# Rotating keys, values and the meta block of a head group with VectorE's 32-block transpose and GpSimd transfers through DRAM

## The chip, the cores and the metric

The kernel runs on one core of one Trainium2 chip. The metric is the device time in microseconds (us) of one execution. A core has a matrix engine (TensorE, PE in the profile; its weight loads are listed as PEld), VectorE (DVE), ScalarE (ACT), GpSimd (POOL) and SyncE (SP), each with its own queue of instructions that it works off in order. Weights come from DRAM by transfers (DMA) that SP issues; GpSimd can issue transfers as well. PE works from SBUF, 128 partitions wide, into PSUM; ACT and DVE bring results from PSUM back to SBUF.

## The reference

One decoder block, width 2048, on 256 tokens with 16 learned meta tokens in front (272 in all). An RWKV-7 path and an attention path with forget gates (FoX), 16 heads of 64 each, run side by side on the same normalised input; their outputs are gated, added and projected, and a SwiGLU layer follows. All is float32.

```python
def _layer(h, ...):
    xn = _rms(h, n1)
    proj = xn @ w_in                       # 2048 x 10704
    z_rwkv, z_fox, z_gate = jnp.split(proj, (RWKV_COLS, RWKV_COLS + FOX_COLS), axis=-1)
    z_prev = jnp.pad(z_rwkv, ((0, 0), (1, 0), (0, 0)))[:, :-1]
    z_rwkv = z_rwkv + (z_prev - z_rwkv) * mu
    y_a = _rwkv7(z_rwkv, ...)              # per head: S = S*w + (S a) b' + v k',  y = S r
    y_b = _fox(z_fox, q_g, k_g, f_bias)    # softmax(q k' * scale + c_q - c_k, causal) v
    g_a, g_b = jnp.split(jax.nn.sigmoid(z_gate), 2, axis=-1)
    h = h + (g_a * (y_a @ w_a) + g_b * (y_b @ w_b)) @ w_o
    gate, up = jnp.split(_rms(h, n2) @ w_gu, 2, axis=-1)
    return h + (jax.nn.silu(gate) * up) @ w_dn
```

## The kernel before

**Precision and weights.** Each float32 matrix product is made of three products of a faster 32-bit type. A weight tile of 128 x 1024 (512 KB) is fetched by SP into `raw` (4 buffers), ACT copies its high part into `wh` (L353), DVE subtracts to get the low part `wl` (L354; 4 buffers each), and PE multiplies both with the activations (L383 to L385, or L459 and L461 where two terms share a matmul). Each weight element is used once, so the chain SP, ACT, DVE, PE runs from start to end of the kernel.

**Stages.** The projection goes head group by head group (four groups g of four heads). For each group the main work is: the RWKV columns k, v, r and the small low-rank products (`rwkv_jobs`, `lora`), the FoX columns q, k, v (`fox_jobs`), then two blocks of gate columns (`gate_jobs`, tile name `zg`). The first group starts some 50 us in and the last group's chain ends at about 560 us. Remaining gate blocks, the branch products, the output projection and the SwiGLU layer follow.

**What sets the order.** PE's order is written out by hand. Beside the main jobs there are background streams, Python generators `rwkv_bg` (L763) and `fox_bg` (L1132), one each per group. After every few main matmuls `slot` (L415) adds the matmuls' nominal time to a clock and, where a stream is due, lets it emit its next step. A stream yields how long it wants to be left alone in nominal ns: the constants `LANE`, `NORM`, `Y_...`, `X_...` at the top of the file. So the small matmuls of one group's recurrence and attention stand between the large ones of the next group's projection. The order on DVE, ACT and POOL is set by the framework's scheduler from priorities and modelled times, with semaphores for every dependence. An engine waits at the first instruction that is not ready, and everything behind it on that engine waits too.

**The steps that the change touches**, per group. `rwkv_bg` builds, from r, k and v after the token-shift (`lerp`, L500; its difference `zd` on POOL at L514, its end on DVE at L517) and the cumulated decay, the tiles `bk` (keys and b vectors, channels on partitions, 128 x 1024; `bk0` for the meta block), `ar`, and the products `NK` (PE `mat`, DVE L835 and L845). The recurrence needs keys and values with tokens on partitions. For that PE turns `bk` by 8 transposes of 128 x 128 against an identity (`trbk`), `v` by 4 (`trv`), and the meta block by 2 (`tr`), all through `pe_tr` (L411 to L413) at L883 to L908, and ACT brings them from PSUM into `BK` (two tags: `bt`), `SV` (`sv`), `BK0` and `SV0` (L891, L900, L905, L907). Then DVE inverts small triangular blocks in `lx` (L921 and L923), `lx` goes through DRAM into `X`, `X0` and `XL`, and the chain of `step` (L939) runs over the chunks with matmuls `rhs`, `u`, `s`, `y`; at its end `yT` is turned back on PE and put into `ya` (one half on ACT, L1050, one on DVE, L1052). `fox_bg` turns v of the attention (`vv`) by 4 PE transposes (`pv`) and its last 32 tokens (`ve`) by one (`pvm`) at L1132 to L1148; ACT scales them into `vt` and `vm`. After that come `biases` (POOL, L1163 to L1166), `scores` (PE `sc`, DVE sum and row maximum L1186, `nm` L1189, ACT exponentials), division (DVE L1203), transposes `ppt` and the product `po` with `vt` and `vm`.

That is 14 + 5 = 19 transposes by the identity per group, 76 in all.

Of the kernel before, what the change touches and what calls it, by code (L numbers as in the profile page):

```python
# [13 lines left out]
ALU = mybir.AluOpType  # L14
# [80 lines left out]
LANE = 24000  # L95
# [6 lines left out]
NORM = 5150  # L102
# [16 lines left out]
Y_AB = 6000  # L119
# [3 lines left out]
Y_TRBK = 1600  # L123
Y_TR0 = 2400
Y_RHS = 1400
Y_U = 1400
Y_XT = 800
Y_QT = 1200
Y_GN = 1400
# [5 lines left out]
def hybrid_block(ctx, tc, A, out, dbg=None):  # L135
# [626 lines left out]

    def rwkv_bg(g, box):  # L763
# [101 lines left out]
        nc.gpsimd.tensor_copy(bk0[:, :, 0, 32:32 + NMETA], vr[:, :, :NMETA])  # L865
# [28 lines left out]
        ps = aux_ps(f"trv{g}")  # L894
        for m in range(2):
            for e in range(2):
                i = 2 * m + e
                pe_tr(ps[:, i * P:(i + 1) * P], vr[:, m, NMETA + e * P:NMETA + (e + 1) * P], ident)
        for cc in range(2):
            nc.scalar.activation(SV[HD:, :, cc::2, :].rearrange("p h i d -> p i h d"),  # L900
                                 ps[hb(cc), :].rearrange("p (i h d) -> p i h d", h=2, d=HD), AF.Copy)
        ps = aux_ps(f"tr0{g}")
        for m in range(2):
            pe_tr(ps[:, m * P:(m + 1) * P], bk0[:, m].rearrange("p x t -> p (x t)"), ident)
        nc.scalar.activation(BK0.rearrange("p h m d -> p m h d"),  # L905
                             ps[:, 0:2 * P].rearrange("p (m h d) -> p m h d", h=2, d=HD), AF.Copy)
# [11 lines left out]
        for s_ in range(31):  # L918
# [20 lines left out]
        def step(c, S, BK, SV, NK, X, Y):  # L939
# [1209 lines left out]
```

## Time and profile before

| | |
|---|---|
| time, median of 3 (lowest to highest) | 1492.32 us (1492.18 to 1492.40) |
| the profiled execution: its time, its span | 1492.06 us, 1490.1 us |
| ACT busy | 844.3 us, 57% of the span |
| POOL busy | 157.0 us, 11% |
| moved by DMA | 307.63 MB, mean 206 GB/s |
| of it read from DRAM, written to it | 286.55 MB, 19.30 MB |

The profiled execution took 0.26 us less than the median, and 1.96 us of its time lie outside the span. The three runs lie within 0.22 us. In the rows that follow, "busy" is the time that an engine executed. Matmuls overlap in PE's pipeline, so the duration of one record is longer than the distance between the starts of two; where the cost of PE work is wanted, starts have to be compared. "Idle before" is the time in which an engine had nothing running just before an instruction of the group, with the instruction that released it.

### The profile page before, as it was taken

What the parts mean: (1) busy time and instruction counts of PE and PEld (TensorE: products, weight loads), DVE (VectorE), ACT (ScalarE), POOL (GpSimd) and SP (SyncE); (2) the same over time, 40 slices, a digit from 0 to 9 for tenths busy, and PEclk for the clock granted to TensorE, in tenths of its full rate; (3) what the DMA queues carried; (4) which work ended last, traced back from release to release, by engine and by line L of the source; (5) the groups of instructions that cost most, each with busy time, mean ns of one, the idle gap of its engine ahead of it and who ended that gap; (6) DMA issues with size and microseconds to landing.
All of it is one profiled execution on the core that took longest, in us unless ns stands there. A gap on an engine that the chain in (4) does not pass through costs nothing.

```text
span 1490.1 us, 27294 instructions
## 1 busy us (share of the span) xinstructions
PE 1480.7 (99%) x10371; PEld 1326.7 (89%) x10371; DVE 1246.3 (84%) x2154; ACT 844.3 (57%) x1255; POOL 157.0 (11%) x273
## 2 busy tenths in 40 slices
PE   9999999999999999999999999999999999999998
PEld 9999999989989888998888999999999988788886
DVE  7888699699789767776778788888898887999898
ACT  7664665575485455554555555555655555565554
POOL 2212202203212010000002000000000002221000
PEclk9999999999999999999999999999999999999999
DMA  8566556646636757767779655675666567988652
GB/s 275 171 178 191 153 146 188 173 140 174 193 114 180 223 148 230 238 219 244 258 252 342 206 176 195 200 244 184 207 230 208 198 213 221 315 265 264 218 198 85
DMA packets 226210, 307.63 MB, mean 206 GB/s; under 512 B 27232, under 2 KB 150128, under 8 KB 226080
## 3 DMA queue, kind: packets, MB, share of 16 engines
q1 hardware_dynamic: 209344, 277.39, 59.9%
q0 software_dynamic: 10688, 22.02, 4.5%
q10 hardware_dynamic: 6048, 6.49, 1.3%
q8 instruction: 81, 1.33, 0.4%
q14 instruction: 49, 0.40, 0.1%
HBM read 286.55 MB, written 19.30 MB: 205 GB/s over the span
## 4 chain that ended last, share of the span: by engine, by line
PE 85%; issue 12%; DVE 1%; DMA 1%; ACT 0%; POOL 0%; SPq 0%; DVEq 0%; POOLq 0%; ACTq 0%
PE zg L459 8%; PE up L459 5%; PE gt L459 5%; PE zg L461 4%; PE dn L1936 4%; PE dn L1935 4%; PE dn L1937 4%; PE up L461 2%; PE f L383 2%; PE gt L461 2%; PE f L385 2%; PE f L384 2%; PE f L459 2%; PE br L383 2%; PE br L384 2%
## 5 line engine op out<-in xcount | busy, mean ns | idle before, releaser
L354 DVE TENSOR_TENSOR wl<-raw,wh 128x1024 fp32r<-128x1024 f32 x268 | 326.6, 1226 | 91.7 <-ACT wh L353 87.1
L353 ACT ACTIVATE wh<-raw 128x1024 fp32r<-128x1024 f32 x268 | 281.7, 1057 | 196.4 <-PE br L384 36.2
L459 PE MATMUL zg<-xhl,wh 128*128 128x512 f32 x512 | 180.1, 398 | 0.0
L459 PE MATMUL gt<-hts,wh 128*128 128x512 f32 x512 | 179.3, 394 | 0.0
L459 PE MATMUL up<-hts,wh 128*128 128x512 f32 x512 | 179.3, 394 | 0.0
L1620 DVE TENSOR_TENSOR wl<-raw,wh 128x1024 fp32r<-128x1024 f32 x128 | 155.1, 1219 | 20.8 <-ACT wh L1617 16.4
L1617 ACT ACTIVATE wh<-raw 128x1024 fp32r<-128x1024 f32 x128 | 133.6, 1051 | 51.9 <-PE gt L459 11.9
L461 PE MATMUL gt<-hts,wl 128*128 128x256 f32 x480 | 134.4, 280 | 0.0
L461 PE MATMUL up<-hts,wl 128*128 128x256 f32 x480 | 134.3, 280 | 0.0
L461 PE MATMUL zg<-xhl,wl 128*128 128x256 f32 x480 | 134.3, 280 | 0.0
L1786 ACT ACTIVATE wh<-fr 128x1024 fp32r<-128x1024 f32 x48 | 50.9, 1061 | 112.9 <-DVE fr L1763 107.9
L459 PEld LDWEIGHTS zg<-xhl,wh 128*128 128x128 f32 x512 | 94.3, 188 | 19.1 <-issue 0.7
L459 PEld LDWEIGHTS up<-hts,wh 128*128 128x128 f32 x512 | 94.5, 188 | 17.2 <-DVE gates L1650 0.2
L459 PEld LDWEIGHTS gt<-hts,wh 128*128 128x128 f32 x512 | 94.5, 188 | 17.0
L1935 PE MATMUL dn<-wh,ach 128*128 128x512 f32 x242 | 95.0, 393 | 0.0
L1936 PE MATMUL dn<-wh,acl 128*128 128x512 f32 x242 | 94.9, 392 | 0.0
L1937 PE MATMUL dn<-wl,ach 128*128 128x512 f32 x242 | 94.7, 392 | 0.0
L461 PEld LDWEIGHTS zg<-xhl,wl 128*128 128x128 f32 x480 | 90.9, 189 | 1.1
L461 PEld LDWEIGHTS gt<-hts,wl 128*128 128x128 f32 x480 | 90.9, 189 | 1.0
L461 PEld LDWEIGHTS up<-hts,wl 128*128 128x128 f32 x480 | 90.9, 189 | 1.0
L1789 DVE TENSOR_TENSOR wl<-fr,wh 128x1024 fp32r<-128x1024 f32 x48 | 58.8, 1224 | 28.8 <-ACT wh L1786 25.6
L528 ACT ACTIVATE wh<-tt 128x1024 fp32r<-128x1024 f32 x44 | 46.7, 1062 | 61.3 <-PE dn L1936 48.3
(774 smaller groups left out, 4118.7 us busy)
## 6 DMA issues: line engine op xcount, KB each, us to landing
raw<-in_w_in_dram SPq DMA_DIRECT2D x160, 512.0 KB
raw<-in_w_gate_up_dram SPq DMA_DIRECT2D x128, 512.0 KB
fr<-in_w_gate_up_dram SPq DMA_DIRECT2D x96, 256.0 KB
raw<-in_w_down_dram SPq DMA_DIRECT2D x44, 512.0 KB
q<-in_w_down_dram SPq DMA_DIRECT2D x44, 512.0 KB
raw<-in_w_o_dram SPq DMA_DIRECT2D x32, 512.0 KB
raw<-in_w_branch_a_dram SPq DMA_DIRECT2D x16, 512.0 KB
raw<-in_w_branch_b_dram SPq DMA_DIRECT2D x16, 512.0 KB
```

The source lines that it names most:

```text
L353: nc.scalar.activation(th, rr, AF.Copy)
L354: nc.vector.tensor_tensor(tl, rr, th.bitcast(F32), op=ALU.subtract)
L383: nc.tensor.matmul(ps, wh, ah, start=first, stop=False)
L384: nc.tensor.matmul(ps, wh, al, start=False, stop=False)
L459: nc.tensor.matmul(ps.rearrange("p (a t) -> p a t", a=2), wh, act, start=first, stop=last)
L461: nc.tensor.matmul(ps[:, :T], wl, act[:, 0, :], start=False, stop=False)
L1617: nc.scalar.activation(w[0], raw[0].rearrange("p (k j c) -> p k j c", k=2, j=1), AF.Copy)
L1620: nc.vector.tensor_tensor(w[1], raw[0].rearrange("p (k j c) -> p k j c", k=2, j=1), w[0].bitcast(F32), op=ALU.subtract)
L1789: nc.vector.tensor_tensor(w[1], raw[0], w[0].bitcast(F32), op=ALU.subtract)
L1935: nc.tensor.matmul(o, a[0], hi, start=first, stop=False)
L1936: nc.tensor.matmul(o, a[1], hi, start=False, stop=False)
L1937: nc.tensor.matmul(o, a[0], lo_, start=False, stop=last)
```

## The change

The 76 transposes of keys, values and meta block leave PE, with ACT's copies out of PSUM (12 per group, the 2 into `ve` among them). In their place, per group:

- DVE runs nine 32 x 32-block transposes (`STREAM_TRANSPOSE`; `turned`): `bt` from `bk`, 128 x 1024; `sv` from `v`, twice 128 x 256; `t0` (meta block), three of 128 x 64; `vt` from `vv`, twice 128 x 256, and its last 32 tokens, 128 x 64. Within each 32 x 32 block, rows and columns are then swapped; the blocks themselves are still in the old place.
- POOL writes each result to DRAM (`bkd` 512 KB, `vd` 256 KB, `t0d` 96 KB, `vtd` 288 KB) and reads it back with the blocks moved: 4 transfers for `bk`, 2 for `SV`, 4 for `BK0`, 1 for `SV0`, 4 for `vv`, 2 for `vm`. These are 4 writes and 17 reads, 21 transfers that POOL issues per group, 84 in all, in rows of 128 B to 1 KB.
- POOL puts the columns in order: two copies into `bt`, four scalings into `vt`, one of `vm`; one more tile to clear (`BK0`), one copy less (`bk0` from v).

In the same edit the last `ya` copies move from DVE to ACT, four small `nm` products per pair of heads become one, `vv` is brought in once with 272 columns, `XL`'s transfers come last, `SV`'s and `vt`'s columns lie in blocks of 32, and some of the streams' delays change.

```diff
-LANE = 24000
+LANE = 25000
-NORM = 5150
+NORM = 7750
-X_DIV = 2600
-X_PT = 2350
-X_PT0 = 5750
+X_DIV = 3600
+X_PT = 3100
+X_PT0 = 6850
-Y_AB = 6000
+Y_AB = 5900
-Y_TRBK = 1600
-Y_TR0 = 2400
+Y_SOLVE = 4000
+V_LAND = 14050
-Y_XT = 800
+Y_XT = 900
-Y_GN = 1400
+Y_GN = 2200
...
+    def turned(tmp, srcs, dram):
+        for dst, src in srcs:
+            nc.vector.transpose(dst, src)
+        nc.gpsimd.dma_start(dram, tmp)
+
+    def rows_of(dram):
+        return dram.rearrange("(a i) b x -> b i a x", i=32)
...
-        nc.gpsimd.tensor_copy(bk0[:, :, 0, 32:32 + NMETA], vr[:, :, :NMETA])
+        BK, SV = (rw.tile([P, 4, 8, 32], F32, tag=t, name=f"{t}{g}", bufs=1) for t in ("bt", "sv"))
...
+        turned(bv, [(BK, bk.rearrange("p m c x (q j) -> p (x q) (m c) j", j=32))], bkd)
+        sv = SV[:, 0:2]
+        turned(sv.rearrange("p b i j -> p b (i j)"),
+               [(sv[:, :, 4 * m:4 * m + 4, :], vr[:, m, NMETA:].rearrange("p (c b j) -> p b c j", b=2, j=32))
+                for m in range(2)], vd)
+        turned(t0.rearrange("p b m j -> p b (m j)"),
+               [(t0[:, x], bk0[:, :, x, :32]) for x in range(2)] + [(t0[:, 2], vr[:, :, :32])], t0d)
...
-        for m in range(2):
-            ps = aux_ps(f"trbk{g}{m}")
-            for c in range(4):
-                pe_tr(ps[:, c * P:(c + 1) * P], bkf[:, 4 * m + c, :], ident)
-            nc.scalar.activation(BK[:, :, 4 * m:4 * m + 4, :].rearrange("p h c d -> p c h d"),
-                                 ps.rearrange("p (c h d) -> p c h d", h=2, d=HD), AF.Copy)
-        yield Y_TRBK
...
-        yield Y_TR0
-
+        yield Y_SOLVE
...
+            if s_ == 7:
+                bkx = bk.rearrange("p m c x t -> p (m c x t)")
+                for b in range(4):
+                    nc.gpsimd.dma_start(bkx[32 * b:32 * b + 32].rearrange("p (a x) -> p a x", a=4), rows_of(bkd)[b])
+                flat = lambda t: t.rearrange("p a i j -> p a (i j)")
+                for b in range(2):
+                    nc.gpsimd.dma_start(flat(SV[HD + 32 * b:HD + 32 * b + 32]), rows_of(vd)[b])
...
+        for h in range(2):
+            nc.gpsimd.tensor_copy(BK[:, h].rearrange("p i (q j) -> p q i j", j=32),
+                                  bkx.rearrange("p (h q i j) -> p h q i j", h=2, q=2, j=32)[:, h])
...
-                if h == cc:
-                    nc.scalar.activation(dst, src, AF.Copy)
-                else:
-                    nc.vector.tensor_copy(dst, src)
+                nc.scalar.activation(dst, src, AF.Copy)
...
-                pe_tr(pv_[:, t * 256 + m * P:t * 256 + (m + 1) * P], vv[:, m, t * P:(t + 1) * P], ident)
-        pe_tr(pvm[:4 * NMETA, :P], ve.rearrange("p m c -> p (m c)"), ident)
...
+        turned(vt.rearrange("p b m j -> p b (m j)"),
+               [(vt[:, t:8:2], vv[:, :, t * P:(t + 1) * P].rearrange("p m (b j) -> p b m j", j=32))
+                for t in range(2)] + [(vt[:, 8], vv[:, :, T - NMETA:])], vtd)
+        yield HOP
+        vb = vv.rearrange("p m l -> p (m l)")[:, :4 * P].rearrange("p (a x) -> p a x", a=4)
+        for b in range(4):
+            nc.gpsimd.dma_start(vb[32 * b:32 * b + 32], vtd[:, 2 * b:2 * b + 2].rearrange("(a i) t x -> i a (t x)", i=32))
...
+        yield V_LAND
         while len(ready) < 2 or not gate_done:
             yield X_V
...
+                nc.gpsimd.tensor_scalar(vt[:, t, m].rearrange("p h (q j) -> p h q j", j=32), v5[:, t, m],
+                                        rsk[:, t:t + 1], None, op0=ALU.mult)
+        nc.gpsimd.tensor_scalar(vm[:2 * NMETA], vm[:2 * NMETA], rsz, None, op0=ALU.mult)
...
-                    nc.vector.tensor_scalar(nm, nm, -1.0, r, op0=ALU.mult, op1=ALU.mult)
...
+            nc.vector.scalar_tensor_tensor(nm, nm, -1.0, hr.rearrange("p (t m h) -> p t m h", t=2, m=2)[:, :, m, :],
+                                           op0=ALU.mult, op1=ALU.mult)
```

Three places show what this does to the order. In the rows, the number behind a name tells apart tiles of one name, and the last figures are the shape.

On PE, before, where the first group's gate columns (`zg`) are multiplied while the group's keys and values are turned:

```order
L461 MATMUL zg_1_1585<-xhl,wl 128x256
L413 MATMUL trbk_1654<-ident,bk_1301 128x128 x4
L413 MATMUL trbk_1660<-ident,bk_1301 128x128 x4
L459 MATMUL zg_1_1585<-xhl,wh 128x512
L461 MATMUL zg_1_1585<-xhl,wl 128x256
```

The same place of the changed kernel, behind the sums `bs` that stand ahead of it in both:

```order
L900 MATMUL bs_1621<-rkl_1314,bones 128x256
L459 MATMUL zg_1_1600<-xhl,wh 128x512
L461 MATMUL zg_1_1600<-xhl,wl 128x256
L459 MATMUL zg_1_1600<-xhl,wh 128x512
L461 MATMUL zg_1_1600<-xhl,wl 128x256
```

The transposes are gone and nothing has taken their place; the two other places of the group (`pv` with `pvm`, and `trv` with `tr`) are emptied likewise.

On POOL, before, between the first group's bonus term `bo` and the difference `zd` of the second group's first key block, with what each waits for in brackets:

```order
L879 TENSOR_SCALAR bo_1600<-bo_1600,vcol 128x256 [waits DVE_49]
L1163 TENSOR_SCALAR b_1701<-bias_1700,cq,hs_999 128x144 [waits DMAHW4_49]
...
L1166 TENSOR_TENSOR bias_1700<-bias_1700,cmask 128x2x128 [waits Pool_49]
L805 MEMSET bk_2919 128x256 [waits PE_49]
L505 MEMSET z 128x1 [waits Activation_49]
L514 TENSOR_TENSOR zd<-z 128x272 [waits DVE_49,Activation_49,Pool_49]
```

The same stretch of POOL in the changed kernel, whose line numbers are higher by 15 to 25 there:

```order
L902 TENSOR_SCALAR bo_1615<-bo_1615,vcol 128x256 [waits DVE_49]
L931 DMA SV_1511<-t0d_1518 32x4x64 [waits DMASW5_49]
L766 DMA vtd_1647<-vt_1646 128x576 [waits DMASW6_49,DVE_49]
L940 COPY bt_1509<-bk_1300 128x2x8x32 [waits DMASW2_49,DMASW3_49,DMASW1_49,DMASW0_49]
L940 COPY bt_1509<-bk_1300 128x2x8x32
L813 MEMSET bk_2850 128x256 [waits PE_49]
L1155 DMA vv_997<-vtd_1647 32x4x128 [waits DMASW7_49,DMASW6_49,Activation_49]
...
L1166 TENSOR_SCALAR vt_1646<-vv_997,rsk 128x128 [waits DMASW2_49,DMASW7_49,DMASW1_49,DMASW0_49]
L1166 TENSOR_SCALAR vt_1646<-vv_997,rsk 128x128 x3
...
L514 TENSOR_TENSOR zd<-z 128x272 [waits DVE_49,Pool_49]
```

Ahead of `zd` now stand transfers, and instructions that wait for landings (the waits named DMASW are for transfers that POOL itself issued); the `biases` have moved behind the scalings of `vt`.

On DVE, before, at the change from the first to the second group: a weight subtraction, root steps of small vectors, the products `NK`, and the next weight subtraction:

```order
L354 TENSOR_TENSOR wl<-raw,wh 128x1024
L295 TENSOR_TENSOR ht<-hr_2496 128x8
L296 SCALAR_TENSOR_TENSOR ht<-hs_2495,ht 128x8
L297 SCALAR_TENSOR_TENSOR ht<-ht 128x8
L835 TENSOR_TENSOR NK_3028<-mat_3111,mup 128x512
L298 TENSOR_SCALAR ht<-ht 128x8
L835 TENSOR_TENSOR NK_3028<-mat_3112,mup 128x512
L299 TENSOR_TENSOR hr_2496<-ht,hr_2496 128x8
L845 TENSOR_TENSOR NK_3029<-mat_3123,mup 80x2x16
L845 TENSOR_TENSOR NK_3029<-mat_3124,mup 80x2x16
L1090 TENSOR_TENSOR hs_2495<-hs_2495,hr_2496 128x8
L354 TENSOR_TENSOR wl<-raw,wh 128x1024
```

The end of the same stretch in the changed kernel; the weight subtraction ahead of it stands 52 rows before its last row:

```order
L765 STREAM_TRANSPOSE sv_3114<-v_1883 128x2x128
L298 TENSOR_SCALAR ht<-ht 128x8
L297 SCALAR_TENSOR_TENSOR gt<-gt 128x8
L765 STREAM_TRANSPOSE t_3117<-bk_2850 128x64
L299 TENSOR_TENSOR hr_2445<-ht,hr_2445 128x8
L298 TENSOR_SCALAR gt<-gt 128x8
L765 STREAM_TRANSPOSE t_3117<-bk_2850 128x64
L299 TENSOR_TENSOR s_2914<-gt,s_2914 128x8
L1104 TENSOR_TENSOR hs_2444<-hs_2444,hr_2445 128x8
L843 TENSOR_TENSOR NK_2977<-mat_3081,mup 128x512
L843 TENSOR_TENSOR NK_2977<-mat_3082,mup 128x512
...
L354 TENSOR_TENSOR wl<-raw,wh 128x2x512
```

Five transposes of the change (the large `bt`, two `sv`, two of the meta block) and the first group's four score sums (L1203 there) and divisions (L1223, L1225) have moved into one stretch with the second group's `NK`. In the two later changes of group the matching stretch holds five transposes too, but its end stands only 28 and 27 rows behind the weight subtraction ahead of it.

More of the change, by code (lines that the diff above doesn't have):

```diff
@@ L863, in rwkv_bg @@
             nc.gpsimd.tensor_copy(N12[h * HD:h * HD + 32], NK[0:32, h, :, 32:64])
-        nc.gpsimd.tensor_copy(bk0[:, :, 0, 32:32 + NMETA], vr[:, :, :NMETA])
+        BK, SV = (rw.tile([P, 4, 8, 32], F32, tag=t, name=f"{t}{g}", bufs=1) for t in ("bt", "sv"))
+        SV0 = s2t(f"SV0{g}").rearrange("p x y d -> p (x y d)").rearrange("p (a m j) -> p a m j", a=4, m=2)
+        BK0 = s2t(f"BK0{g}")
+        t0 = rw.tile([P, 8, 32], F32, tag="xt", name=f"t0{g}", bufs=1)[:, :6].rearrange("p (b m) j -> p b m j", m=2)
+        nc.gpsimd.memset(SV0, 0.0)
+        nc.gpsimd.memset(BK0, 0.0)
+        bkd, vd, t0d = (dp.tile([P, n, w], F32, tag=t, name=f"{t}{g}", bufs=2)
+                        for t, n, w in (("bkd", 4, 256), ("vd", 2, 256), ("t0d", 3, 64)))
+        bv = BK.rearrange("p b i j -> p b (i j)")
+        turned(bv, [(BK, bk.rearrange("p m c x (q j) -> p (x q) (m c) j", j=32))], bkd)
[5 more added lines that the diff above has]
+               [(t0[:, x], bk0[:, :, x, :32]) for x in range(2)] + [(t0[:, 2], vr[:, :, :32])], t0d)
         for h in range(2):
@@ L931, in rwkv_bg @@
                 nc.sync.dma_start(X[h * HD + 32 * q:h * HD + 32 * q + 32, :, 32 * q:32 * q + 32], d2v[h, q, :32])
+        for h in range(2):
+            nc.sync.dma_start(X0[h * HD:h * HD + 16, :, 0:32], d2[32:, :16].rearrange("(h m) r t -> h r m t", h=2)[h])
+        for h in range(2):
             nc.sync.dma_start(XL[h * HD:h * HD + 32], d2v[h, 1, :32][:, 1::2, :])
-            nc.sync.dma_start(X0[h * HD:h * HD + 16, :, 0:32], d2[32:, :16].rearrange("(h m) r t -> h r m t", h=2)[h])
         yield LANE - (N_FIRST if g == 0 else 0), ("chain", 1)
@@ L1148, in fox_bg @@
         while len(ready) < 2 or not gate_done:
             yield X_V
+        vt = vt.rearrange("p b m j -> p (b m j)")[:, :4 * P].rearrange("p (t m h d) -> p t m h d", t=2, m=2, h=2)
+        v5 = vb.rearrange("p (h q) (t m j) -> p t m h q j", q=2, t=2, m=2)
+        for t in range(2):
+            for m in range(2):
+                nc.gpsimd.tensor_scalar(vt[:, t, m].rearrange("p h (q j) -> p h q j", j=32), v5[:, t, m],
+                                        rsk[:, t:t + 1], None, op0=ALU.mult)
@@ L1179, in scores @@
                           start=True, stop=True)
+            nm = fx.tile([P, 2, 2], F32, tag="nm", name=f"nm{g}{m}", bufs=2)
             for t in range(2):
-                n = nq[t]
                 for h in range(2):
-                    s = sc_t[h, t]
-                    nm = fx.tile([P, 1], F32, tag="nm", name=f"nm{g}{m}{h}{t}", bufs=4)
                     bb = b1[:, h, :] if t == 0 else bias[:, h, :]
-                    nc.vector.tensor_tensor_reduce(s[:, :n], pss[h][:, cq_[t]], bb, 1.0, -3.0e38, op0=ALU.add,
-                                                   op1=ALU.max, accum_out=nm)
-                    r = hr[:, qc(t, m, h)]
-                    nc.vector.tensor_scalar(nm, nm, -1.0, r, op0=ALU.mult, op1=ALU.mult)
-                    nc.scalar.activation(s[:, :n], s[:, :n], AF.Exp, scale=r, bias=nm,
+                    nc.vector.tensor_tensor_reduce(sc_t[h, t][:, :nq[t]], pss[h][:, cq_[t]], bb, 1.0, -3.0e38,
+                                                   op0=ALU.add, op1=ALU.max, accum_out=nm[:, t, h:h + 1])
+            nc.vector.scalar_tensor_tensor(nm, nm, -1.0, hr.rearrange("p (t m h) -> p t m h", t=2, m=2)[:, :, m, :],
+                                           op0=ALU.mult, op1=ALU.mult)
+            for t in range(2):
+                for h in range(2):
+                    s = sc_t[h, t][:, :nq[t]]
+                    nc.scalar.activation(s, s, AF.Exp, scale=hr[:, qc(t, m, h)], bias=nm[:, t, h:h + 1],
                                          accum_out=sums[:, 2 * t + h:2 * t + h + 1])
```

75 lines of the change are left out of this document (28 added, 47 removed).

## The prediction

> **What bounds the kernel now.** I read the head of the page first: the span, the busy times, and the shares by engine of the chain of work that ended last.
>
> ```profile
> span 1490.1 us, 27294 instructions
> ...
> PE 1480.7 (99%) x10371; PEld 1326.7 (89%) x10371; DVE 1246.3 (84%) x2154; ACT 844.3 (57%) x1255; POOL 157.0 (11%) x273
> ...
> PE 85%; issue 12%; DVE 1%; DMA 1%; ACT 0%; POOL 0%; SPq 0%; DVEq 0%; POOLq 0%; ACTq 0%
> ```
>
> PE is busy throughout and ends the chain. The change touches only the stretch from 60 to 560 us, so next I read there what PE waited for (us, times, longest):
>
> ```profile
> PE u3-1_7162 L409 <- ACT R3-1_7136 L951: 0.2, 1, 0.2
> PE X L409 <- ACT QT L1010: 0.2, 1, 0.2
> ```
>
> 0.4 us in 500: whatever leaves PE's queue there comes off the time in full, unless something that PE now never waits for becomes late. Who is nearest to that? A window at the change from group 1 to 2 (length, busy times of PE, PEld, DVE, ACT, POOL, clock, DMA share, GB/s):
>
> ```profile
> 200.00:250.00 50.00, 50.00 (x427) 46.53 (x426) 47.42 (x120) 29.87 (x52) 12.08 (x19) 1.00 0.58 161
> ```
>
> DVE, 47.4 of 50 us. It gets work from the change; ACT (29.9) loses some; POOL (12.1) gets most of the work but is idle three quarters of the time. What shields PE from DVE is the four buffers of the weights:
>
> ```profile
> L353 ACT ACTIVATE wh<-raw 128x1024 fp32r<-128x1024 f32 x140 | 147.7, 1057 | 91.3 <-PE f L384 23.1 <-PE zg L459 21.7 <-PE v L384 16.5
> ```
>
> ACT's idle time ahead of these copies, 60 to 560 us, ended mostly with a PE matmul that gave a buffer back: the buffers are full most of the time.
>
> **What goes: 76 transposes on PE.** All instructions of that line (duration min/median/max in ns, first and last start):
>
> ```profile
> L413 PE MATMUL trbk<-ident,bk x32: 270/272/273, 115.0 to 466.0; 128*128 128x128 f32 x32
> L413 PE MATMUL pv<-ident,vv x16: 271/272/273, 113.3 to 467.8; 128*128 128x128 f32 x16
> L413 PE MATMUL trv<-ident,v x16: 270/272/274, 117.6 to 468.7; 128*128 128x128 f32 x16
> L413 PE MATMUL tr<-ident,bk x8: 272/272/273, 118.0 to 468.9; 128*128 128x128 f32 x8
> L413 PE MATMUL pvm<-ident,ve x4: 273/273/273, 113.8 to 467.9; 128*64 128x128 f32 x4
> ```
>
> 272 ns is the length of one record in the pipeline, not what PE gains without it. That is read from starts, in PE's timeline (start, us, line, tile):
>
> ```profile
> 113.00 0.39 PE L459 MATMUL zg<-xhl,wh 128*128 128x512 f32 x1
> 113.23 0.28 PE L461 MATMUL zg<-xhl,wl 128*128 128x256 f32 x1
> 113.35 0.60 PE L413 MATMUL pv<-ident,vv 128*128 128x128 f32 x4
> 113.79 0.27 PE L413 MATMUL pvm<-ident,ve 128*64 128x128 f32 x1
> 113.81 0.48 PE L459 MATMUL zg<-xhl,wh 128*128 128x512 f32 x1
> 114.13 0.28 PE L461 MATMUL zg<-xhl,wl 128*128 128x256 f32 x1
> ...
> 114.95 1.03 PE L413 MATMUL trbk<-ident,bk 128*128 128x128 f32 x8
> 115.74 0.47 PE L459 MATMUL zg<-xhl,wh 128*128 128x512 f32 x1
> ```
>
> `pv` and `pvm` push the next `zg` from 113.35 to 113.81, 0.46 us; and that `zg` matmul takes 0.32 to the next start where an undisturbed one takes 0.23 (113.00 to 113.23), 0.09 more for the interruption. So 0.55. `trbk`: 0.79 + 0.09 = 0.88, about 0.10 per transpose. `trv` and `tr`, six at 0.095 and one restart: 0.66. Per group 2.09, four groups **8.4 us**, 0.56% of the time. The Trainium skill ("TensorE: Matmul & The Clock Gate", Part 4: PE-mode transpose) puts a 128 x 128 transpose in a kernel at about 275 ns. Its figure is the record's length here; by it the gain would be 76 x 0.275 = 20.9 us, and as an estimate of the time, 1471. The starts, 0.10 apart, speak against it.
>
> **What DVE gets and loses**, per group. Groups of its instructions from 60 to 560 us (busy us, mean ns | idle before):
>
> ```profile
> L354 DVE TENSOR_TENSOR wl<-raw,wh 128x1024 fp32r<-128x1024 f32 x139 | 170.8, 1232 | 36.6 <-ACT wh L353 33.6 <-PE QT L409 2.9
> ...
> L1186 DVE CUSTOM_DVE_ANT_0 sc<-sc,bias 128x272 f32<-128x272 f32 x16 | 6.9, 433 | 0.0
> L1189 DVE TENSOR_SCALAR nm<-nm,hr 128x1 f32<-128x1 f32 x32 | 6.1, 210 | 0.5
> ...
> L1203 DVE TENSOR_SCALAR sc<-sc,sums 128x256 f32<-128x256 f32 x16 | 4.9, 346 | 0.0
> ...
> L1000 DVE STREAM_TRANSPOSE XT<-X 128x256 f32<-128x256 f32 x4 | 1.8, 442 | 3.4 <-DMA X<-d 3.4
> ```
>
> A 32-block transpose of 128 x 256 takes 0.44 us; of 128 x 1024 I take 1.24, as the subtraction of that size; of 128 x 64, 0.24 (between the 0.21 of `nm`, one element per partition, and 0.44). Added: 1.24 + 2 x 0.44 + 3 x 0.24 + 2 x 0.44 + 0.24 = 4.0. Gone: six of eight `nm`, 6 x 0.21 = 1.3, and two `ya` copies of 256 elements, 0.4 each by the 0.43 and 0.35 of the rows of that size: 0.8. Net **+1.9 us**, in a group of some 110. With 36.6 us of idle time ahead of the `wl` alone that is covered on the average. What counts is where it is bunched. ACT, with 12 copies less and two more, gets no later.
>
> The bunch is the stretch on DVE between two `wl`, at the change to group 2. Before, from its timeline:
>
> ```profile
> 212.12 1.21 DVE L354 TENSOR_TENSOR wl<-raw,wh 128x1024 fp32r<-128x1024 f32 x1
> ...
> 221.44 1.21 DVE L354 TENSOR_TENSOR wl<-raw,wh 128x1024 fp32r<-128x1024 f32 x1
> ```
>
> From the end of the first (213.33) to the start of the second are 8.1 us, with another `wl` of 1.2 in between, so 6.9 of other work. The order puts that third `wl` behind and adds: `bt` 1.24, two `sv` 0.88, two of the meta block 0.48, four score sums at most 4 x 0.43, four divisions at most 4 x 0.35, and small ones that cancel. Sum 12.6. With the next `wl` itself, 13.8 us without new weights. PE uses 139 tiles in 500 us, 3.6 us each: four full buffers last 14.4 us, three 10.8. The stall is between 0 and 3.0; I take **2**, nearer to three: DVE, busy 47.4 of 50 us there, is the engine that would be behind. At the two later changes of group the order has 28 and 27 rows in place of 52: five transposes 2.6, the next `wl` 1.2 and some twenty rows of about 0.2 (as `nm`), 7.8 in all. That is hidden with three full buffers (10.8), and costs 0.6 with two (7.2). I take **0.6** each, the upper end, since buffers may still be short after what came before.
>
> **What POOL gets.** It issues 21 transfers per group; the nearest rows are another one's issues and landings, in ns and us, then its own idle time in the first group:
>
> ```profile
> L2062 POOL DMA_DIRECT2D hh<-hhd x8: 537/549/552, 1280.3 to 1365.3; - x8
> ...
>   DMA to landing us min/median/max: 4.1/6.4/7.9
> ```
>
> ```profile
> 145.92 0.64 POOL L514 TENSOR_TENSOR zd<-z 128x272 f32<-128x272 f32 x1 [24.83 <-DVE z L506]
> ```
>
> POOL waits 24.8 us there for DVE, and `zd` of the second group's keys is the next thing that others need from it. Into this gap go: `SV0`'s read, `vtd`'s write and six reads, 8 x 0.55 = 4.4; two copies into `bt`, four scalings and `vm`, some 4 (0.64 each by the row of `zd`); and two stands, one for the landing of `vtd` and one for that of its reads, 4.1 to 7.9 each, so 8 to 16. The thirteen issues ahead of `bo`, 7 us, fall partly into waits that POOL has there already; I count half, 3. In all 20 to 28, the middle 24: it just fits the 24.8, cost 0, at the upper end 3 us late, which the buffers hide. In the first group there is one more place: two `zd` of r stand behind a read of `vd` that waits for the write's landing, 4.1 at least, with DVE's L517 behind them, and `wl` behind that. Between 0, with full buffers, and 4.1, with none, I take **0.3**, near the covered end. The tiles that the reads fill are wanted tens of us later (chain and `po`), so direct waits cost nothing. The moving operands in two pieces of 32 columns, and streams set 1 to 3 us later, I take at 0: nothing in the rows prices them; 2 us either way go into the range.
>
> The Trainium skill has a rule against this change ("SBUF — State Buffer", A bandwidth-pool intuition that's wrong): a transfer that GpSimd issues has to wait for a port that VectorE holds, about 3100 ns under a VectorE copy where it takes 620 alone. By the trace: the issues quoted above, 552 ns at most beside a DVE 84% busy over the span, agree with the short figure; the row under rival (d) may be the long one.
>
> **Sum.** -8.4 + 2 + 2 x 0.6 + 0.3 = -4.9. The moved attention steps may interrupt `zg` more often, 0.09 each time, or less often: between 0 and a dozen times, 1.1 us; I take 0.5. That makes -4.4. 1492.06 - 4.4 = 1487.66, so **1487.7**. The profiled execution lies 0.26 under the median; I add nothing for that. Own range 1485.5 to 1490: the first stall at 0 gives 1485.7, at 3.0 with 1.1 of interruptions and 0.6 more on POOL 1489.9.
>
> **Rivals.**
>
> (a) *Full gain*: all buffers are full at the bunches, no stall. 1492.06 - 8.4 = **1483.7**. For it: PE's waits of 0.4 us in 500. Against: 13.8 of 14.4 us leave no room.
>
> (b) *DVE becomes the bound*: near the changes of group it has 2.6 us of 50 left. If every net us of its work reaches PE, +1.9 x 4 = 7.6, and the time is **1491.3**. Against: 36.6 us of its idle time ended with ACT's `wh`, that is, with PE's buffers.
>
> (c) *POOL is late for the next group's keys, slower than before*. The place is `zd`, on which DVE's L517 waits, with `wl` behind it (for k now, us, times, longest):
>
> ```profile
> DVE k L517 <- POOL z L505: 4.7, 6, 1.0
> ```
>
> If each landing takes not 4.1 to 7.9 but 15 us, POOL needs 4.4 + 4 + 30 + 3 = 41.4 in a gap of 24.8, 16.6 late; the buffers hide 9.6 (three tiles at 3.6 less a `wl`). 7 us at each of three changes of group: -8.4 + 21 = +12.6, **1504.7**. It decides from 11.5 us per landing ((24.8 + 9.6 - 11.4) / 2). For it: these reads come in short rows, 128 B to 1 KB, and four at a time. Against: 7.9 at the most above.
>
> (d) *POOL is held up by DVE* in each transfer that it issues:
>
> ```profile
> L814 POOL COPY dc<-dd x4: 1053/1710/3423, 88.4 to 437.4; 128x8 f32<-128x8 f32 x4
> ```
>
> One copy of 8 columns took 1.05 to 3.42 us. If each of the 21 transfers of a group took 2.4 more, 50 us join the 24 in a gap of 24.8: 49 late, 40 past the buffers, three times, less 8.4: about **1604**. Against: the 552 ns at most. It is what the port rule of the Trainium skill, above, would do here.
>
> (e) The gain per transpose is the record's 272 ns: 20.7 us, **1471**.
>
> **Chances.** Forecast 0.36, (a) 0.30, (b) 0.17, (c) 0.13, (d) 0.03, (e) 0.01. The measurement can tell some 0.2%, 3 us, from no change: 1489.3 and 1495.3 are the edges. Faster: (a), (e) and most of the forecast, 0.62; slower: (c) and (d) 0.14 to 0.16, the lower since a late POOL may cost less than 7 us; same: (b) and the forecast's upper end, 0.24. The range goes from 1482.5, (a) with 1.2 of the unpriced 2 us, to 1495, (b) with the 2 us and the interruptions; it leaves out (c) to (e), 0.17.
>
> **What would show it.** PE's row of waits from 60 to 560 us: right, if it holds 2 to 5 us, mostly for `wl` near 220 us; if still 0.4, it is (a); if waits for `wl` are spread over all groups, (b); if DVE's L517 waits for POOL (1.0 us at the longest for k now) by many us, (c); POOL issues well over 0.55 us, (d). DVE's row for `bt` should read about 1.24 us. Wrong at the root: if PE's sum of busy time falls by much less than 8 us with no wait, the moved steps interrupt more than counted.

## The result, and the profile after

| | before | changed kernel |
|---|---|---|
| median time (lowest to highest) | 1492.36 us (1492.18 to 1492.76) | 1503.62 us (1500.97 to 1506.58) |
| ratio, 95% interval | | 1.0076 (1.0055 to 1.0096) |
| profiled execution | 1492.06 us | 1506.58 us |

Slower, by 11.3 us by the medians; the profiled execution, the slowest of the changed kernel's, is 14.5 us over that of before. Its page (span; busy times; engines' shares of the chain that ended last):

```profile
span 1504.9 us, 27299 instructions
...
PE 1483.7 (99%) x10295; PEld 1325.2 (88%) x10295; DVE 1259.7 (84%) x2158; ACT 829.9 (55%) x1215; POOL 229.4 (15%) x385
...
PE 62%; issue 13%; DVE 4%; DMA 1%; ACT 1%; SPq 0%; POOL 0%; DVEq 0%; ACTq 0%; POOLq 0%
```

PE's matmuls fell by 76, but its busy time rose by 3.0 us; and a gap between busy time and span of 21.2 us stands where 9.4 stood. What PE waited for from 60 to 560 us (us, times, longest):

```profile
PE QT L409 <- DVE XT L1018: 8.1, 4, 2.6
PE k L385 <- DVE wl L354: 2.2, 1, 2.2
PE s2-1_5609 L409 <- DVE SV L983: 0.5, 1, 0.5
PE u3-1_7172 L409 <- ACT R3-1_7146 L969: 0.5, 1, 0.5
PE zg L461 <- DVE wl L354: 0.4, 1, 0.4
PE y L409 <- DVE sv L985: 0.2, 1, 0.2
```

Four stops, one per group, at `QT`, the first chain product that needs `X` from the triangular solve. A stop is not over when PE goes on. The first group's in PE's timeline (start, us, [idle before]):

```profile
154.68 0.29 PE L384 MATMUL v<-xhl,wh 128*128 128x272 f32 x1
154.81 0.29 PE L385 MATMUL v<-xhl,wl 128*128 128x272 f32 x1
157.66 0.45 PE L409 MATMUL QT<-XT,N 32*32 32x32 f32 x32 [2.57 <-DVE XT L1018]
157.94 0.31 PE L409 MATMUL u0-1_2201<-R0-1_2172,X 32*32 32x64 f32 x8
158.19 0.60 PE L383 MATMUL v<-xhl,wh 128*128 128x272 f32 x1
158.58 0.43 PE L384 MATMUL v<-xhl,wh 128*128 128x272 f32 x1
158.81 0.43 PE L385 MATMUL v<-xhl,wl 128*128 128x272 f32 x1
```

The same matmuls start 0.13 us apart ahead of the stop and 0.23 behind it, until about 162 us. The windows' clock column (third from the end) says why:

```profile
150.00:160.00 10.00, 7.43 (x93) 6.93 (x92) 6.58 (x12) 2.51 (x4) 2.71 (x6) 0.91 0.64 155
160.00:170.00 10.00, 10.00 (x126) 9.22 (x126) 5.40 (x13) 4.51 (x9) 1.14 (x3) 0.92 0.74 219
280.00:290.00 10.00, 7.47 (x118) 6.78 (x118) 6.20 (x15) 2.96 (x8) 2.66 (x5) 0.83 0.63 175
520.00:530.00 10.00, 7.44 (x99) 5.72 (x98) 4.85 (x11) 3.81 (x9) 0.00 (x0) 0.67 0.79 226
530.00:540.00 10.00, 10.00 (x86) 8.14 (x86) 4.58 (x10) 3.54 (x7) 0.00 (x0) 0.99 0.45 118
```

The missing part of the clock, times 10 us each, is 6.8 us in all: 1.7 behind the first stop, 1.7 behind the second, 3.4 behind the fourth (2.06 us, and 0.5 at `u` right after). The third, 0.9 us, left the clock alone. It is such lost time that shows as "busy".

Why is `XT` late? The solve's path in the first group, on SP and DVE, before (the products `NK` go to DRAM, come back as `ln`, and the first step of the solve):

```profile
105.13 0.87 SPq L854 DMA_DIRECT2D d<-NK  x2
...
109.32 1.12 SPq L860 DMA_DIRECT2D ln<-d  x3
...
114.72 0.33 DVE L921 TENSOR_TENSOR lt<-lx,ln 108x31 f32<-108x31 f32 x1
```

and after:

```profile
105.42 0.88 SPq L862 DMA_DIRECT2D d<-NK  x2
...
112.24 1.12 SPq L868 DMA_DIRECT2D ln<-d  x3
...
117.73 0.59 DVE L917 TENSOR_TENSOR lt<-lx,ln 108x31 f32<-108x31 f32 x1
```

The transfer starts 0.3 us later, the issue of `ln`, which waits for its landing, comes 2.9 us later (6.8 us behind that of `d` where it was 4.2), and the solve starts 3.0 later. The same for all groups, from the two traces (us). `bs` is a product ahead of the solve; the solve runs from the start of its first step `lt` to the end of its last, `lx`; PE's arrival is the start of the matmul ahead of `QT`; `XT` is ready at its end:

| group | last `bs` on PE to first `lt` | the solve | its end to `XT` | last `bs` to PE's arrival at `QT` | `XT` ready ahead of PE |
|---|---|---|---|---|---|
| 1 before, after | 3.9, 6.8 | 28.4, 28.7 | 9.6, 10.6 | 44.8, 43.8 | 2.5, -2.7 |
| 2 | 7.0, 8.6 | 26.2, 35.2 | 10.1, 10.6 | 48.5, 52.2 | 4.8, -2.7 |
| 3 | 6.6, 9.0 | 26.3, 30.2 | 10.0, 9.4 | 48.1, 47.9 | 4.8, -1.1 |
| 4 | 6.6, 9.1 | 26.2, 31.7 | 11.1, 9.0 | 47.6, 48.0 | 3.3, -2.2 |

(The last column is the fourth number less the first three and less the 0.45 us of `XT`, within rounding. The recorded expectations below count from the wait in DVE's queue ahead of the first `lt`, up to 3.0 us before `lt` itself; so their starts are earlier and their solves longer than these.) From the last `bs`, `XT` is ready 4.2 to 11.2 us later than before, and PE arrives between 1.0 us earlier and 3.8 later. So a lead of 2.5 to 4.8 us was used up, mostly by a solve that starts 1.6 to 2.8 us later and lasts 0.3 to 9.0 longer. The later landing alone doesn't explain the later start in groups 2 to 4: in both kernels DVE is busy with other work right up to the first `lt` there.

The solve's own 62 steps on DVE take 15.1 to 15.5 us in all before and 16.8 to 18.3 after. One of them, in group 2:

```profile
260.77 1.62 DVE L917 TENSOR_TENSOR lt<-lx,ln 108x91 f32<-108x91 f32 x1
262.42 0.25 DVE L919 TENSOR_TENSOR lx<-lx,lt 108x91 f32<-108x91 f32 x1
```

and this what POOL does meanwhile:

```profile
260.85 0.73 POOL L1184 TENSOR_TENSOR b<-b,cmask 128x256 f32<-128x256 f32 x1
261.55 0.72 POOL L1185 TENSOR_TENSOR bias<-bias,cmask 128x256 f32<-128x256 f32 x1
```

The step takes 1.62 us beside POOL's two, and the step behind it, of the same size, 0.25. The Trainium skill ("SBUF — State Buffer", Who interferes with whom) says that a VectorE instruction with two SBUF inputs contends with a GpSimd instruction that reads SBUF; the trace agrees. But this is the smaller part of the 9.0 us that group 2's solve gained: 3.1 us are its steps, 2.7 are four more operations of DVE's that fall between them, and 3.6, where before there was no such wait, are DVE's waits for ACT's `wh`, the longer one here:

```profile
240.88 1.23 DVE L354 TENSOR_TENSOR wl<-raw,wh 128x1024 fp32r<-128x1024 f32 x1 [2.63 <-ACT wh L353]
```

### The profile page after: what moved, and what is told of

Its sections match the earlier page's. It is cut to its first block, busy times and chain, and to the rows that moved or that the text cites. A ratio compares the mean times of both kernels' runs of the same rounds, so it can differ in the third digit from the quotient of the medians.

```text
span 1504.9 us, 27299 instructions
## 1 busy us (share of the span) xinstructions
PE 1483.7 (99%) x10295; PEld 1325.2 (88%) x10295; DVE 1259.7 (84%) x2158; ACT 829.9 (55%) x1215; POOL 229.4 (15%) x385
## 4 chain that ended last, share of the span: by engine, by line
PE 62%; issue 13%; DVE 4%; DMA 1%; ACT 1%; SPq 0%; POOL 0%; DVEq 0%; ACTq 0%; POOLq 0%
PE zg L459 5%; PE up L459 5%; PE gt L459 5%; PE dn L1955 4%; PE dn L1954 4%; PE dn L1956 4%; PE zg L461 2%; PE up L461 2%; PE gt L461 2%; PE br L383 2%; PE br L384 2%; PE br L385 2%; PE wo L1414 2%; PE wo L1416 2%; PE wo L1415 2%
```

## Experiments

Stop time is PE's idle time from 60 to 600 us (0.4 in the kernel before), clock loss the sum over its windows of 10 us of the missing clock times 10. Both are of one profiled execution.

| run | median us | ratio to before, 95% | stops us | clock loss us |
|---|---|---|---|---|
| changed kernel | 1503.62 | 1.0076 (1.0055 to 1.0096) | 12.2 | 6.8 |
| no_tr | 1484.88 | 0.9951 (0.9936 to 0.9966) | 2.4 | 0 |
| before_lane18 | 1518.82 | 1.0174 (1.0159 to 1.0189) | 17.7 | 8.5 |
| lane31 | 1501.17 | 1.0059 (1.0044 to 1.0074) | 8.8 | 5.1 |
| lane275 | 1503.15 | 1.0070 (1.0054 to 1.0086) | 9.8 | 3.4 |
| lane29_ab9 | 1517.39 | 1.0162 (1.0145 to 1.0178) | 17.7 | 8.5 |
| tr_back | 1504.19 | 1.0084 (1.0067 to 1.0101) | 5.2 | 1.7 |
| fox_on_pe | 1495.45 | 1.0016 (1.0006 to 1.0025) | 6.8 | 1.7 |
| rwkv_on_pe | 1495.61 | 1.0018 (1.0008 to 1.0027) | 2.7 | 0 |
| no_bkd | 1494.55 | 1.0018 (1.0008 to 1.0027) | 5.5 | 0 |
| order_on_act | 1516.31 | 1.0158 (1.0139 to 1.0177) | 18.4 | 8.5 |
| fox_on_pe_lane27 | 1506.51 | 1.0093 (1.0078 to 1.0108) | 10.8 | 6.8 |
| no_tr_lane27 | 1498.03 | 1.0036 (1.0024 to 1.0048) | 9.5 | 6.8 |
| no_tr_both27 | 1495.65 | 1.0023 (1.0012 to 1.0033) | 6.7 | 1.7 |
| fox_early25 | 1502.78 | 1.0069 (1.0053 to 1.0086) | 10.5 | 6.9 |
| fox_early27 | 1503.10 | 1.0071 (1.0054 to 1.0088) | 12.7 | 3.4 |
| small_edits | 1491.46 | 0.9994 (0.9984 to 1.0003) | 0 | 0 |
| fox_only24 | 1490.71 | 0.9988 (0.9979 to 0.9997) | 0 | 0 |
| fox_only245 | 1491.91 | 0.9998 (0.9989 to 1.0006) | 1.2 | 0 |

**What the 76 transposes are worth, and what a stop costs.** `no_tr`, on the kernel before:

```diff
-                pe_tr(ps[:, c * P:(c + 1) * P], bkf[:, 4 * m + c, :], ident)
...
+                                 bkf[:, 4 * m:4 * m + 4].rearrange("p c (h d) -> p c h d", d=HD), AF.Copy, scale=0.0)
```

> The kernel before with the 76 transposes left out (ACT's copies keep their number and sizes but read SBUF and are scaled to zero: recurrence and attention values are not computed properly). It measures the gain on PE alone. By the starts in the trace: 8.4 us less, about 1484 (1483 to 1485). Rival: the record's length counts, 20 us less, 1472; or the places stay interrupted, 1487 or more.

Ratio 0.9951, some 7.3 us less, with 2.4 us of stops in it:

```profile
PE QT L409 <- DVE XT L989: 2.4, 2, 1.2
```

So the 8.4 us are about right (7.3 + 2.0 more stops than before = 9.3, the interval being 2.2 us wide to either side). Counted from the last `bs`, PE comes to `QT` 2.1 us earlier in each group, 8.5 in all. But `XT`, too, is ready 1.2 to 2.5 us later there, with nothing added; the lead at `QT` is used up by both, in two of the four groups. `before_lane18`, the kernel before:

```diff
-LANE = 24000
+LANE = 18000
```

> The kernel before with LANE 18000 in place of 24000 and nothing else: PE comes to QT some 6 to 7 us earlier, while XT was ready 2.5 to 4.8 us ahead before. Theory: four stops of 2 to 4 us at QT, each followed by 2 to 4 us lost to a lower granted clock, so 1492 + 12 + 10 = about 1514 (1504 to 1520). Rival: a stop costs its own length only and PE catches up in the later slack, 1492 + 12 = 1504 or less, clock 1.00.

```profile
PE QT L409 <- DVE XT L1000: 13.6, 4, 5.4
```

26.5 us over before by the median, stops 17.3 more and clock 8.5: 25.8. Stops and clock price it nearly in full, without anything of the change.

**Coming later to QT.** Three runs of the changed kernel with another start of the chain, `lane31`, `lane275` and `lane29_ab9`:

```diff
-LANE = 25000
+LANE = 31000
```

```diff
-LANE = 25000
+LANE = 27500
```

```diff
-LANE = 25000
+LANE = 29000
...
-Y_AB = 5900
+Y_AB = 9000
```

> The changed kernel with LANE 31000 in place of 25000: PE comes to the chain's first steps some 6 us later. Theory A (PE waits 8.1 us in 4 stops at QT, because the triangular solve in lx and the landing of X end later than before while PE arrives no later; and each stop of over 2 us is followed by a few us at a lower granted clock): the stops at QT go and with them the slow clock, 1503.6 - 8 - 7 = about 1488 (1485 to 1491). Rival B (the loss is spread over late weight parts on a DVE that GpSimd holds up): QT's stops go, but PE waits for wl instead, time stays at or above 1498.

> The changed kernel with LANE 27500, halfway towards 31000, where QT's stops were gone but mat stopped for bk (6.9 us in 3). Theory: QT's stops fall to 0 to 2 us; whether mat stops then decides between 1488 to 1494 (it doesn't) and 1498 to 1502 (each shift of the chain meets another step).

> The changed kernel with LANE 29000 in place of 25000 and Y_AB 9000 in place of 5900: PE comes later both to QT and to the products mat that waited for bk with LANE 31000 (6.9 us in 3). Theory: no stop of over 1 us is left, the granted clock stays at 1.00, and the gain of the removed transposes shows less some 4 us of late weight parts and interruptions: 1486 to 1490. Rival (DVE or GpSimd has too much to do, whatever the places): a new stop appears elsewhere, 1495 or above.

All three missed. The times are nearer to those of their rivals (1498 or above, 1498 to 1502, 1495 or above), though `lane275` opened other stops than the `mat` that it asked about: `y` and `u` at 2.0 us each, `s0` 1.7. In `lane31` the stops at `QT` are gone, as expected, but PE's first row is a new one:

```profile
PE mat L409 <- DVE bk L817: 6.9, 3, 2.3
```

In `lane29_ab9` that one is gone, `QT` still stops for 1.9 us, `y` waits 4.9 us for DVE's `sv`, and `u` 3.3 and 3.0 us for ACT. The expectation that a stop is cured by its own delay fell: each of the three shifts brought stops at other steps.

**Which part delays the solve.** `tr_back` puts 18 of each group's 19 transposes back on PE, into PSUM that nobody reads:

```diff
+                pe_tr(ps[:, c * P:(c + 1) * P], bkf[:, 4 * m + c, :], ident)
+        yield 1600
```

> The changed kernel with the transposes back on PE at their old places (18 of 19 per group, into PSUM that nobody reads), everything else as changed. Theory (PE comes to QT before XT is ready, and a stop costs more than the work that was taken away): PE comes some 1.5 us later per group to QT, the stops fall from 8.1 to 3 us or less, the slow clock goes, and the time falls although PE has 8 us more to do: 1495 to 1500. Rival (the added work on DVE and GpSimd is what costs, wherever PE is): the 8 us come on top, 1510 or above.

1504.19 us: neither. Eight us more work on PE cost nothing net, as stops and clock loss fell from 19.0 to 6.9; but it didn't get faster. `fox_on_pe` and `rwkv_on_pe` undo one half each:

```diff
+                pe_tr(pv_[:, t * 256 + m * P:t * 256 + (m + 1) * P], vv[:, m, t * P:(t + 1) * P], ident)
...
-        yield V_LAND
```

```diff
+                pe_tr(ps[:, c * P:(c + 1) * P], bkf[:, 4 * m + c, :], ident)
...
-                    nc.gpsimd.dma_start(bkx[32 * b:32 * b + 32].rearrange("p (a x) -> p a x", a=4), rows_of(bkd)[b])
```

> The changed kernel with the attention's V part as before (five transposes per group on PE, no vtd, vv and vm transfers, scaling on ACT). If the POOL work inside the solve (vt scalings, transfers of vtd) stretches lx on DVE (theory A1), QT's stops fall below 3 us in sum and the time to about 1490 to 1495 (2.2 us of the gain is given up). If the transfers of bk, vd and t0d make the landing of the solve's own transfers late (theory A2), the stops stay at 6 us or more and the time at 1500 or above.

> The changed kernel with the RWKV part as before (14 transposes per group on PE, no bkd, vd, t0d transfers); the attention's V part stays turned off PE. A2: the transfers ahead of the solve land as early as before (ln about 3 us after d), QT's stops go, 1487 to 1492. A1: the solve stays stretched by POOL's scalings and transfers of vtd, stops of 3 us or more in sum remain, 1495 or above.

Both halves count. With the RWKV part turned (`fox_on_pe`) the issue of `ln` comes 5.5 to 6.3 us after that of `d` (2.6 to 4.2 before) and the first `lt` 7.3 to 12.1 after `bs`; the solve's steps take 15.2 to 15.5 us as before, and its solves, 26.6 to 30.3 us, are longer only by other work of DVE's between the steps. With the attention's part turned (`rwkv_on_pe`) `d` to `ln` is 2.7 to 4.2 as before, `lt` comes 5.5 to 7.5 after `bs`, later than before in the first group alone, and the solves last 28.1 to 32.3, their steps 15.9 to 17.1. So the RWKV part makes `ln` and the start late, the attention's part makes the steps and the solve long. `no_bkd` leaves out the write and reads of `bkd`:

```diff
-        turned(bv, [(BK, bk.rearrange("p m c x (q j) -> p (x q) (m c) j", j=32))], bkd)
+        turned(bv, [(BK, bk.rearrange("p m c x (q j) -> p (x q) (m c) j", j=32))], None)
```

> The changed kernel without the write of bkd and its four reads per group (1 MB per group; the keys of the recurrence are zero, so its values are not computed properly); the 32-block transposes and the copies into bt stay. If these transfers delay the solve's own (ln lands late, first lt 6 to 8.5 us after bs where it was 4), first lt comes at 4 to 5 us after bs, QT's stops fall from 8.1 to 3 us or less and the time to 1490 to 1496. If not, 1500 or above.

The time came as expected, its reason not: `lt` stays late (6.6 to 9.1), `d` to `ln` at 3.8 to 6.6. The large transfer alone is not what holds up `ln`; whether the small ones (`vd`, `t0d`, rows of 128 to 256 B) do, or the transposes on DVE, wasn't tried. The traces point at the transfers: in the changed kernel's first group POOL issues three reads of `t0d` and one of `bkd` from 105.32 us on, beside SP's `d` at 105.42, in `no_bkd` four of `t0d` from 103.95, `d` coming at 105.69, and none in `rwkv_on_pe`, where `ln` follows `d` as early as before. `order_on_act` puts in order on ACT:

```diff
-            nc.gpsimd.tensor_copy(BK[:, h].rearrange("p i (q j) -> p q i j", j=32),
...
+            nc.scalar.activation(BK[:, h].rearrange("p i (q j) -> p q i j", j=32),
...
-                nc.gpsimd.tensor_scalar(vt[:, t, m].rearrange("p h (q j) -> p h q j", j=32), v5[:, t, m],
...
+                nc.scalar.activation(vt[:, t, m].rearrange("p h (q j) -> p h q j", j=32), v5[:, t, m],
```

> The changed kernel with the putting in order (two copies into bt, four scalings into vt, one of vm per group) on ScalarE in place of GpSimd; transfers stay. If GpSimd's SBUF work beside the solve stretches lx (theory A1), the solve falls from 29.1, 36.0, 30.6 and 33.0 us to 29 to 31 in all groups, QT's stops fall by 2 us or more, and the time to 1495 to 1500. If it is the biases and transfers alone, solve and time stay (1500 to 1507).

A miss, outside both forecasts: solves of 29.1 to 34.0 us, and PE 10.2 us behind `wl` and `wh`. Yet the stretch that it was meant to remove is gone, as the solve's steps take 14.4 to 15.2 us. In its place DVE waits within the solve for ACT, which now has the work: 3.5, 4.9 and 5.8 us for `zg` (L465) in groups 2 to 4, and for `wh` in the first.

**Which distance opens the stops.** `fox_early25` and `fox_early27` are the changed kernel without `V_LAND`, the scalings issued late instead, with most other delays of the kernel before; the second moves chain and attention by 2000 more:

```diff
-BIAS = 35400
+BIAS = 36400
...
-        yield V_LAND
...
+                        nc.gpsimd.tensor_scalar(vt[:, tt, mm].rearrange("p h (q j) -> p h q j", j=32), v5[:, tt, mm],
```

```diff
-LANE = 25000
+LANE = 27000
...
-BIAS = 35400
+BIAS = 38400
```

`fox_on_pe_lane27` is `fox_on_pe` with `LANE = 27000`. `no_tr_lane27` and `no_tr_both27` are `no_tr` with the first, and with both, of:

```diff
-LANE = 24000
+LANE = 27000
...
-BIAS = 35400
+BIAS = 38400
```

> The changed kernel with the attention's steps back at the place that they had before relative to the chain: no V_LAND, the scalings of vt and vm issued later (behind the divisions, ahead of the product that needs them), NORM and the X_ and Y_ delays as before, LANE 25000 and BIAS 36400, both 1000 over before. Theory (the 14000 of V_LAND took the attention's steps apart from the chain's: 10 more interruptions of the main work, score sums beside the next group's transposes on DVE): main work is interrupted 92 times in place of 102, the unexplained 4 us go; QT's stops stay at 4 us or more as the solve still ends late: 1492 to 1498. Rival: the place of the attention's steps doesn't matter, 1501 or above.

> As fox_early25, with LANE 27000 and BIAS 38400: chain and attention together another 2000 later, so PE comes to QT after XT is ready. Theory: QT's stops go to under 2 us, no other stop of over 1 us opens as the two streams keep their distance: 1484 to 1489, faster than both kernels. Rival: the chain, 3000 later than before, meets the next group's steps on DVE and new stops open, 1493 or above.

> The changed kernel with the attention's V part on PE as before and LANE 27000. With LANE 25000 PE stopped 6.8 us in all, 2.8 at QT. Theory: QT's stops go, 1487 to 1492 (14 of 19 transposes gone, 6 us, less the stops that are left). Rival: shifting the chain opens other stops, 1495 or above.

> The kernel before without the 76 transposes (left out as in no_tr, the values are not computed) and with LANE 27000 in place of 24000. With LANE 24000 PE still stopped 2.4 us at QT, as it comes there some 2 us earlier per group. Theory: with 27000 the stops go and the whole 8.4 us are seen: 1483.9 by the median of 1492.3, at most 1484.5. Rival: moving the chain opens a new stop, 1485 or above.

> The kernel before without the 76 transposes (left out as in no_tr, values not computed), LANE 27000 and BIAS 38400, so that chain and attention move together by 3000. With LANE alone at 27000 it took 1498.0 with 9.5 us of stops at y and X. Theory (distance between the two streams is what opened them): stops under 2 us, 1482 to 1485. Rival (the distance to the next group's main work): 1490 or above.

All five missed; each time is the one that its rival named. `no_tr_lane27` took back 13 us with not one turned block in it, only a chain that starts 3000 nominal ns later: `y` waits for DVE 6.0 us, `X` for ACT 2.4. `fox_on_pe_lane27` meets the same two, 5.4 and 3.4. Moving chain and attention together (`no_tr_both27`) still leaves 5.2 us at `y`, which speaks for the distance to the next group's main work. In `fox_early25` the part of the time that stops and clock don't explain fell from 4.3 us to 1.0 (1492.06 - 8.4 + 10.1 + 6.9 = 1500.7, its profiled execution took 1501.7), in `fox_early27` it was 3.9 again. How much of this part the traces explain comes at the end of the next section.

**What is left.** `small_edits` is the kernel before with the `ya` copies and the `nm` product of the change:

```diff
-                if h == cc:
-                    nc.scalar.activation(dst, src, AF.Copy)
-                else:
-                    nc.vector.tensor_copy(dst, src)
+                nc.scalar.activation(dst, src, AF.Copy)
```

`fox_only24` is the changed kernel with the RWKV part back on PE as in `rwkv_on_pe`, the late scalings of `fox_early25`, and the delays of the kernel before; `fox_only245` adds 500 to `LANE` and `BIAS`.

> The kernel before with the two small edits alone: the last ya copies on ScalarE, four nm products in one. They take 2 us per group off DVE, which is not the bound: 1491.5 to 1493, no stop of over 1 us. Rival: an edit of this size already shifts the steps, 1495 or above.

> Only the attention's V part is turned off PE (5 of 19 transposes per group, 2.2 us in all by the starts); its steps keep the places that they had before (no V_LAND, scalings issued later), the RWKV part and all delays as before, LANE 24000; the two small edits stay. PE comes to QT only 0.55 us earlier per group and the solve lies beside fewer GpSimd operations. Theory (stops come from lost margins, and here they are kept): stops of 1 us or less in all, 1489.5 to 1491.5, faster than both kernels. Rival: any shift opens stops, 1493 or above.

> As fox_only24 with LANE 24500 and BIAS 35900, which gives QT back the half microsecond. Theory: as fox_only24 or up to 1 us less, 1489 to 1491.5. Rival: the chain's later steps meet the next group's on DVE, 1493 or above.

`fox_only24` is the one complete version faster than both kernels (`no_tr` leaves the transposes out): 0.9988 (0.9979 to 0.9997), about 1.8 us under before and 13 under the change. Its row from 60 to 600 us:

```profile
60.00:600.00 540.00, 540.00 (x4741) 492.59 (x4739) 445.07 (x1056) 314.84 (x590) 132.23 (x189) 1.00 0.61 180
```

PE never stops and the clock is whole; 2.2 us were to be had by the starts. `small_edits` may hold part of it (0.9994, not clear of 1), and 500 more of delay already gives a stop at `u` and no gain that can be told.

## Why the prediction was wrong

**The step that failed** is "so direct waits cost nothing", with "streams set 1 to 3 us later, I take at 0" and "2 us either way". I looked for what PE "now never waits for" in DVE's weight parts and in POOL's `zd`, not in the chain's own path: `NK`, its landing `ln`, the solve on DVE, `X`, `XT`, `QT`. The row `DVE STREAM_TRANSPOSE XT<-X` stood in the prediction with its idle time, "3.4 <-DMA X<-d", as a price for a transpose; it said that DVE stood waiting for this very landing (1.5 us in the first group, 1.9 in the fourth), so that there any delay of the solve goes straight to `XT`. In the changed kernel, from 60 to 560 us, the row reads:

```profile
L1018 DVE STREAM_TRANSPOSE XT<-X 128x256 f32<-128x256 f32 x4 | 1.8, 445 | 10.2 <-DMA X<-d 10.2
```

PE's lead over `XT` was never computed. It was 2.5 to 4.8 us. The removal itself takes 2.1 us per group of it (`no_tr`); in the changed kernel other delays give PE most of that back or more, and the stops come from `XT`, ready 4.2 to 11.2 us later than before. The 14050 of `V_LAND`, which moves the whole attention stream, was passed over as "1 to 3 us".

**The second error** was to price a stop at its length. In the changed kernel 6.8 us of clock came on top of 11.8 us of added stops. **The third** was the size of one term, the interruptions: 0.5 was taken, of 1.1 at most, and the traces show 2.9 (below).

Point by point:
- The gain, -8.4: right (`no_tr`), as long as the streams stay where they were. With it rival (e), 20.7 us by the record's length, is refuted, and rival (a), no stall at all, by the stops.
- The late `wl` at the change to group 2, 2: 2.2 + 0.4 came, but at 265 us, among group 3's key weights, not at the bunch near 220; that the size agrees is luck. The bunch itself came, 11.9 us from the start of one `wl` copy to the next's, and the buffers held. The 2 x 0.6 of the later groups did not come.
- DVE's durations: 1.234 us for `bt` against 1.24; right.
- POOL's gap: ahead of `zd` of the next keys POOL stood idle for 10.2 us, until DVE's `z` was there, and DVE's L517 waited 0.8 us at most: right. Rival (c), whose 1504.7 is near the measured time by chance, is refuted as a mechanism.
- Rival (d): the issues took 0.54 to 0.72 us, where it needed 2.4 more; refuted. The contention ran the other way: beside POOL's work the solve's steps on DVE came to 16.8 to 18.3 us.
- Moving operands in two pieces at 0: right; 112 starts between `rhs` matmuls sum to 3.68 us in both traces.
- Rival (b): refuted; PE waits for DVE's weight parts for 2.2 + 0.4 us in all.

For the profiled execution the sum now reads 1492.06 - 8.4 + 11.8 + 6.8 = 1502.3, and 4.3 us are missing to the measured 1506.6. Two differences between the traces of `no_tr` and of the changed kernel, from 60 to 620 us, come to about that. Main matmuls (those on `wh` and `wl`) give way to small ones 98 times in the kernel before and 86 times in `no_tr`, but 98 times again in the changed kernel: the moved steps interrupt twelve times more, and the starts of the main matmuls take 2.9 us more for it. And the products `y`, `rhs`, `po`, `s` and `fk` take 2.0 us more; why they do stays open.

## What to carry to other kernels

Where a bound engine's order is written by hand, time taken from it is time taken from the lead of everything that it meets later: for each product list when its last operand is ready and when the engine arrives, and subtract the saving, and what the change adds to the operand's path, from that lead before counting the gain. A stop of some two us cost from nothing to 3.4 us of clock on top of its length here. Work that moves to an idle engine is not free where its transfers or its reads of SBUF fall beside the path that feeds the bound one.

## What the runs showed that I had not expected

- Where the granted clock falls between 60 and 600 us in these traces, it falls to 0.50 for 3.41 us or for twice that: in the changed kernel at 158.2, 284.5 and 523.4 us, which lie 37 and 70 times 3.41 us apart. Whether a stop costs clock does not go by its length alone: 2.57 us at `QT` cost 1.7, 2.17 at 265 us nothing; in `no_tr_lane27` a stop of 1.60 us at 453 us cost 1.7, in `before_lane18` one of 2.53 at 278 nothing. The Trainium skill ("TensorE: Matmul & The Clock Gate", Part 1: The HAM clock gate) has a free-running window of 3.4 us, and half the clock after at least one idle window; these traces agree on the window's length and the half clock, but stops of 1.60 us, less than half a window, sufficed. That a stop's place within the window decides fits the traces and is not shown.
- With the same program the time varied by 5.6 us (1500.97 to 1506.58) where that of before varied by 0.6 in the same session. Stops that cost clock in one execution and not in the next would do this; as only one of them was traced, it is not shown.
- A 32-block transpose of 128 x 1024 takes 1.234 us, what a subtraction of that size takes.
